# A two-layer hybrid decoder trunk on one core: weights fetched two groups ahead, queries and keys copied out of PSUM, two tiles transposed by DMA

## The chip, the core and the metric

The kernel runs on one core of a Trainium2 chip. The core has five engines, each with a queue of its own that it works off in order: TensorE (PE in the profile: matmuls, and PEld for its weight loads), VectorE (DVE), ScalarE (ACT), GpSimd (POOL) and SyncE (SP, which here only issues transfers). Sixteen DMA engines move data. Operands lie in SBUF; matmuls write to PSUM, of which this kernel uses banks of 128 x 512 float32. The metric is the device time of one execution in microseconds.

## The reference, cut

Two layers; a sequence of 512 tokens with 2048 features, float32. Each layer:

```python
h = rmsnorm(x, norm_g);  proj = h @ w_in            # 2048 x 7696
cv_h, cv_b, cv_c, cv_g, sb_q, sb_k, sb_v, sb_g, gl_q, gl_k, gl_v, gl_g, gl_lr = split(proj)
y_conv = cv_b * (causal conv of width 3 over cv_c * cv_h, + bias) * silu(cv_g)
q, k = rmsnorm per head of 128 (sb_q), (sb_k)       # 8 heads
w = exp(log_sigmoid(z) + later)                     # z = q k^T, strictly causal; later: the sum of
y_sb = (w @ sb_v) * silu(sb_g)                      #   log_sigmoid(-z) over later keys of the row
g = log_sigmoid(gl_lr @ gla_w_up + gla_b_up) / 16
y_gla = rmsnorm(gated linear attention(gl_q, gl_k, gl_v, g)) * silu(gl_g)    # 4 heads
x = x + concat(y_conv, y_sb, y_gla) @ w_out         # 2048 x 2048
```

## The kernel before

**Splitting.** Every float32 operand of a large matmul is split into two float16 parts (hi and lo), and three products (hi hi, hi lo, lo hi) take the place of one float32 product.

**Groups.** `specs` lists the column groups of 256 in the order of their use: per layer 6 groups for linear attention (GLA: values, one with the 16 low-rank columns, queries, keys, two gates), 4 for the first half of the convolution, 16 for stick-breaking attention (four times values, gate, queries, keys, for two heads each), 4 for the rest of the convolution, and 8 of `w_out`. A group is 192 matmuls of 256 columns or 96 of 512. Each is fetched and prepared in two halves of 1024 rows, h = 0 and 1:

- `fetch` issues the transfer on SP into a buffer of the pool `stage` (tile `st`, 3 buffers, so one and a half groups);
- `wmax` (L322) squares the half on ACT and sums (tile `junk` takes the squares); `wscale` (L332 to L353) makes a power of two from the sums, on POOL and DVE;
- `whi` (L393) writes the hi part on ACT, `wlo` (L400) the lo part on DVE, into pool `wpool` (tiles `wh`, `wl`, 3 buffers each). `wlo` is the last reader of the staged half.

`weights()` is called at the head of each group's matmuls; it calls `load` for the group itself if that isn't done, and for the next one.

**Matmuls.** `project_cols` (L558 to L560) makes a group's output by columns, `project_toks` (L566 to L568) by tokens, in two PSUM banks out of three (`psp`), `project_by_token` (L591) one token tile after the other, for the first two groups of a layer and for the last of the first layer.

**Order.** But for the start, where the order of ACT and DVE is written out by hand, a scheduler of the framework sets each engine's order at build time from its own model of time and from priorities; `high_priority` lifts what is called in it. Semaphores then hold each instruction back until its data are there.

**GLA.** For each of two head pairs (`p`), seven levels of VectorE and ACT work (L760 to L778: exponentials, splits L724 and L733 on ACT, L725 and L734 on DVE) feed small matmuls (L739); then L817 and L818 split the carried attention, and L830 applies it to the values. These stand among the next groups' matmuls on PE.

**Stick-breaking attention.** `attend` leaves four pieces per two heads (`scores` and `values` of each) that `go()` starts one by one within the following groups. `scores` ends in L956 (exponential, ACT), L959 and L960 (hi and lo) and four DMA transposes on SP (L962, tile `th`), which `values` needs for L978. For queries and keys, ACT squares each 128 x 128 block out of PSUM with an accumulated sum (L1023, eight a group), `rsqrt` follows on ACT and DVE, and DVE multiplies from PSUM into `raw` (L1032 queries, L1040 keys); only then are the group's banks free. `raw` is split into `qp` and transposed by DMA (L1050).

**Change of layer.** In the last group of `w_out`, `finish` (L1070) writes a token tile's new x, and `xprep` prepares it for the next layer: `xnorm`, `xgain` (L446, both halves), `xhigh` (eight float32 transposes on PE, L456, and the hi part out of PSUM on ACT, L458), `xlow` (L465, the lo part on DVE). The results `xh`, `xl` are what the next layer's matmuls read.

Of the kernel before, what the change touches and what calls it, by code (L numbers as in the profile page):

```python
# [6 lines left out]
F16 = mybir.dt.float16  # L7
# [10 lines left out]
P = 128  # L18
# [16 lines left out]
def hybrid_trunk(ctx, tc, x, norm_g, w_in, conv_w, conv_b, sb_qn_g, sb_kn_g,  # L35
# [30 lines left out]
    def sm(n, tag, bufs=None):  # L66
        return small.tile([P, n], F32, tag=tag, name=nm(tag), bufs=bufs)

    def wk(shape, tag, bufs=None, dt=F32):
        return work.tile(shape, dt, tag=tag, name=nm(tag), bufs=bufs)  # L70
# [33 lines left out]
    epst = const.tile([P, 1], F32, tag="epst", name="epst")  # L104
    V.memset(epst, EPS)

    colno = wk([P, P], "gy", 1)
    V.tensor_tensor_scan(colno, ones.to_broadcast([P, P]), ones.to_broadcast([P, P]), -1.0, ALU.mult, ALU.add)
    parno = wk([P, 32], "raw", 1)
    V.transpose(parno, colno[:, :32])  # L110
# [176 lines left out]
    cursor = [0]  # L287

    def load(i):
        if i < 3:  # L290
            load_(i)
        else:
            with tc.high_priority():
                load_(i)

    staged, peak, scales = {}, {}, {}

# [19 lines left out]
    def wmax(i, h):  # L317

        n = sum(c[1] for c in specs[i][2])
        if h == 0:  # L320
            peak[i] = sm(2, "wm")
        S.activation(junk(HK * n).rearrange("p (k n) -> p k n", k=HK), staged[i][h][:, :, :n], AF.Square,  # L322
                     accum_out=peak[i][:, h:h + 1])
# [51 lines left out]
    def whi0(h, q, eng):  # L375
# [9 lines left out]
        else:  # L385
            V.tensor_scalar(wh[:, ks, :GW], staged[0][h][:, ks, :GW], scales[0][0], None, ALU.mult)

    def whi(i, h):
        n = sum(c[1] for c in specs[i][2])
        wh = wpool.tile([P, HK, GX], F16, tag="wh", name=nm("wh"))  # L390
        wl = wpool.tile([P, HK, GX], F16, tag="wl", name=nm("wl"))
        for ks, s_ in wparts(i, h):
            S.activation(wh[:, ks, :n], staged[i][h][:, ks, :n], AF.Copy, scale=s_)  # L393
        loaded[i][0].append((wh, wl))

    def wlo(i, h):
# [5 lines left out]

    def load_(i):

        fetch(i)
        for h in range(2):
            wmax(i, h)
        wscale(i)
        for h in range(2):
            whi(i, h)  # L410
            wlo(i, h)

    def weights():

        i = cursor[0]
        cursor[0] += 1
        for j in (i, i + 1):
            if j < len(specs) and j not in loaded:
                load(j)
        return loaded.pop(i)  # L420

    fetch(0)
# [47 lines left out]

    def xprep(l, t, dst):

        xnorm(l, t)
        for h in range(2):
            xgain(t, h)
            xhigh(t, h, dst)
            xlow(t, h, dst, False)

    def halves(tag):

# [61 lines left out]
    for l in range(depth):  # L542
# [53 lines left out]
        def gate(ps, u, mx=None):  # L596

            g = wk([P, 2, seq], "g")
            for c in range(2):
                y = wk([P, seq], "gy", 1)  # L600
                S.activation(y, ps[c], AF.Copy, scale=u)
                a = wk([P, seq], "ga")
                S.activation(a, y, AF.Abs)
                S.activation(a, a, AF.Exp, scale=-1.0)
                S.activation(a, a, AF.Ln, bias=1.0)
                V.scalar_tensor_tensor(a, y, 0.0, a, ALU.min, ALU.subtract)
                S.activation(a, a, AF.Exp)
                V.tensor_tensor(g[:, c, :], y, a, ALU.mult)
            if mx is not None:
                V.tensor_reduce(mx, g, AX.XY, ALU.max, apply_absolute_value=True)  # L610
            return g
# [55 lines left out]
        for p in range(2):  # L667
# [4 lines left out]
            S.activation(a, gp, AF.Abs, bias=bcol)  # L672
            S.activation(a, a, AF.Exp, scale=-1.0)
            S.activation(a, a, AF.Ln, bias=1.0)
            r_ = wk([P, seq], "gy", 1)
            S.activation(r_, gp, AF.Relu, bias=nbu[:, l, p:p + 1], scale=-1.0)
            V.tensor_tensor(a, a, r_, ALU.add)
            for t in range(NT):
# [313 lines left out]
        for j in range(4):  # L992
# [22 lines left out]
            qkT = []  # L1015
            for gain in (None, kg[:, l, :]):
                ps, u = project_toks(xh, xl)
                sq = sm(8, "qs")
                raw = wk([P, NT, GW], "raw", 1)
                for t in range(NT):  # L1020
                    for hh in range(2):
                        o = (t % 2) * GW + hh * P
                        S.activation(raw[:, t, hh * P:(hh + 1) * P], ps[t // 2][:, o:o + P], AF.Square,  # L1023
                                     accum_out=sq[:, 2 * t + hh:2 * t + hh + 1])
                u2 = sm(1, "qu2")
                V.tensor_scalar(u2, u, u, 1.0 / P, ALU.mult, ALU.mult)
                rs = sm(8, "qr")
                rsqrt(rs, sq, u2, 8, "q")
                V.tensor_scalar(rs, rs, u, None, ALU.mult)
                if gain is None:  # L1030
                    for b in range(2):
                        V.tensor_tensor(raw[:, 2 * b:2 * b + 2, :].rearrange("p a (h c) -> p (a h) c", c=P),  # L1032
                                        ps[b].rearrange("p (a c) -> p a c", c=P),
                                        rs[:, 4 * b:4 * b + 4].rearrange("p (a o) -> p a o", o=1).to_broadcast([P, 4, P]),
                                        ALU.mult)
                else:
                    for t in range(NT):
                        for hh in range(2):
                            o = (t % 2) * GW + hh * P
                            V.scalar_tensor_tensor(raw[:, t, hh * P:(hh + 1) * P], ps[t // 2][:, o:o + P],  # L1040
                                                   rs[:, 2 * t + hh:2 * t + hh + 1], gain, ALU.mult, ALU.mult)

                top = 2.0 ** 10 if gain is None else 1.0
                parts = wk([P, 2, NT * GW], "qp", 1, F16)
# [76 lines left out]
```

## Time and profile before

| | |
|---|---|
| median of 3 runs | 1791.44 us (1789.22 to 1795.85) |
| the profiled execution | 1791.4 us |
| its span in the profile | 1789.6 us |
| granted TensorE clock, mean | 0.996 |
| busy: PE / DVE / ACT / POOL | 1742.9 / 1049.7 / 1085.9 / 55.1 us |
| moved by DMA | 202.61 MB, 113 GB/s on average |

A row of a group of instructions reads: line, engine, operation, tile written <- tiles read, shapes, count | busy us, mean ns of one | idle time of the engine just before them, and what ended most of it. A row of waits reads: waiting instruction <- what released it: us in total, times, longest. A row of the timeline: start us, us, instruction, and in brackets the idle time before it. A row of stages: start and end, length, then busy us (and instructions) of PE, weight loads, DVE, ACT, POOL, then granted clock, DMA share, GB/s. Times are from the span's start.

### The profile page before, as it was taken

The numbers are of one execution on the slowest core, as the hardware profiler recorded it, in microseconds if no ns is written. First come the engines' busy times: TensorE is split into PE (matmuls) and PEld (weight loads), VectorE is DVE, ScalarE is ACT, GpSimd is POOL, SyncE is SP. The second block draws the span as 40 slices with busy tenths as digits, with TensorE's granted clock in tenths as the row PEclk, the third lists the DMA queues.
The fourth block names the chain that finished last, engine by engine and source line by source line (L and its number), as shares of the span: only waits on it lengthen the run. The fifth ranks groups of instructions, "written<-read, shape, count | busy, mean of one in ns | idle before, by whom it ended". The sixth has DMA issues, their size and how long they took to land. (4 is left out here: it accounts for less than half of the span.)

```text
span 1789.6 us, 30839 instructions
## 1 busy us (share of the span) xinstructions
PE 1742.9 (97%) x12878; PEld 1238.4 (69%) x12878; DVE 1049.7 (59%) x1991; ACT 1085.9 (61%) x1652; POOL 55.1 (3%) x104
## 2 busy tenths in 40 slices
PE   8999999999999999999999999999999999999999
PEld 6644456777777754788985454568686778548888
DVE  7556677656565647544463566875666565564323
ACT  8557576567676766555555674775766666655431
POOL 2000000000000000000010000000000000000000
PEclk9999999999999999999999999999999999999999
DMA  6322222243535355444423322223444435444441
GB/s 216 118 95 94 86 80 83 83 119 106 137 92 151 86 150 123 143 148 144 142 89 102 117 73 71 95 80 98 123 119 121 98 108 124 117 124 142 142 142 48
DMA packets 257675, 202.61 MB, mean 113 GB/s; under 512 B 84658, under 2 KB 256764, under 8 KB 257024
## 3 DMA queue, kind: packets, MB, share of 16 engines
q1 hardware_dynamic: 248528, 191.19, 37.4%
q10 hardware_dynamic: 9008, 9.45, 1.6%
q8 instruction: 101, 1.65, 0.4%
q14 instruction: 38, 0.31, 0.1%
HBM read 173.36 MB, written 8.39 MB: 102 GB/s over the span
## 5 line engine op out<-in xcount | busy, mean ns | idle before, releaser
L322 ACT ACTIVATE junk<-st 128x2048 uint8<-128x2048 f32 (+1 forms) x150 | 287.4, 1916 | 339.9 <-DMA st<-in_w_in_dram 244.1
L566 PE MATMUL psp<-wh,m 128*128 128x256 f16 x1664 | 454.3, 273 | 2.4 <-DVE raw L1032 1.7
L567 PE MATMUL psp<-wl,m 128*128 128x256 f16 x1664 | 454.3, 273 | 0.0
L568 PE MATMUL psp<-wh,m 128*128 128x256 f16 x1664 | 454.2, 273 | 0.0
L400 DVE SCALAR_TENSOR_TENSOR wl<-st,ws,wh 128x2048 f16<-128x2048 f32 (+1 forms) x120 | 282.1, 2353 | 147.9 <-ACT wh L393 142.1
L393 ACT ACTIVATE wh<-st,ws 128x2048 f16<-128x2048 f32 (+1 forms) x118 | 236.0, 2001 | 93.8 <-PE psp L568 59.1
L566 PE MATMUL psp<-wh,x 128*128 128x256 f16 x768 | 209.4, 273 | 2.0 <-DVE raw L1032 1.7
L567 PE MATMUL psp<-wl,x 128*128 128x256 f16 x768 | 209.3, 273 | 0.0
L568 PE MATMUL psp<-wh,x 128*128 128x256 f16 x768 | 209.3, 273 | 0.0
L558 PE MATMUL psp<-x,wh 128*128 128x512 f16 x512 | 194.1, 379 | 0.0
L558 PE MATMUL psp<-m,wh 128*128 128x512 f16 x512 | 194.1, 379 | 0.0
L559 PE MATMUL psp<-x,wh 128*128 128x512 f16 x512 | 194.0, 379 | 0.0
L559 PE MATMUL psp<-m,wh 128*128 128x512 f16 x512 | 194.0, 379 | 0.0
L560 PE MATMUL psp<-x,wl 128*128 128x512 f16 x512 | 193.8, 379 | 0.0
L560 PE MATMUL psp<-m,wl 128*128 128x512 f16 x512 | 193.7, 379 | 0.0
L560 PEld LDWEIGHTS <-wl 128*128 128x128 f16 x1024 | 100.2, 98 | 123.2 <-issue 4.5
L559 PEld LDWEIGHTS <-wh 128*128 128x128 f16 x1024 | 100.2, 98 | 117.6 <-issue 2.3
L558 PEld LDWEIGHTS <-wh 128*128 128x128 f16 x1024 | 100.2, 98 | 117.2 <-issue 2.0
L566 PEld LDWEIGHTS <-m 128*128 128x128 f16 x1664 | 163.0, 98 | 23.2 <-DVE raw L1032 2.3
L567 PEld LDWEIGHTS <-m 128*128 128x128 f16 x1664 | 163.0, 98 | 21.0 <-issue 2.1
L568 PEld LDWEIGHTS <-m 128*128 128x128 f16 x1664 | 163.1, 98 | 20.4 <-issue 1.4
L333 DVE TENSOR_SCALAR wq<-wgm 128x1 f32<-128x1 f32 x75 | 16.0, 213 | 263.9 <-POOL wgm L332 263.9
(278 smaller groups left out, 2325.7 us busy)
## 6 DMA issues: line engine op xcount, KB each, us to landing
st<-in_w_in_dram SPq DMA_DIRECT2D x120, 1024.0 KB, 5.3
st<-in_w_out_dram SPq DMA_DIRECT2D x32, 1024.0 KB, 5.8
x<-in_x_dram SPq DMA_DIRECT2D x4, 1024.0 KB
qT<-in_x_dram ACTq DMA_DIRECT2D x8, 512.0 KB, 4.9
qT<-xs ACTq DMA_DIRECT2D x8, 512.0 KB
xs<-x SPq DMA_DIRECT2D x14, 256.0 KB, 4.6
out_dram<-kT SPq DMA_DIRECT2D x14, 256.0 KB, 4.2
th<-za SPq DMA_TRANSPOSE x64, 5.5
```

What stands on the lines that cost most here:

```text
L322: S.activation(junk(HK * n).rearrange("p (k n) -> p k n", k=HK), staged[i][h][:, :, :n], AF.Square, accum_out=peak[i][:, h:h + 1])
L333: V.tensor_scalar(m, gm[:, 0:1], gm[:, 1:2], 2.0 ** -120, ALU.add, ALU.max)
L393: S.activation(wh[:, ks, :n], staged[i][h][:, ks, :n], AF.Copy, scale=s_)
L400: V.scalar_tensor_tensor(wl[:, ks, :n], staged[i][h][:, ks, :n], s_, wh[:, ks, :n], ALU.mult, ALU.subtract)
L558: T.matmul(o, wh[:, kk, cs], xh[:, :, k, :], start=st_, stop=False)
L559: T.matmul(o, wh[:, kk, cs], xl[:, :, k, :], start=False, stop=False)
L560: T.matmul(o, wl[:, kk, cs], xh[:, :, k, :], start=False, stop=en)
L566: T.matmul(o, ah[:, t, k, :], wh[:, kk, :n], start=st_, stop=False, skip_group_check=True)
L567: T.matmul(o, ah[:, t, k, :], wl[:, kk, :n], start=False, stop=False, skip_group_check=True)
L568: T.matmul(o, al[:, t, k, :], wh[:, kk, :n], start=False, stop=en, skip_group_check=True)
```

## The change

`weights()` now calls `fetch` for the group after the next, and `load` for the next group no longer fetches. `load_` puts both squares of a group behind the last `whi` of the group before it on ACT (`issue_after`), and all loads are at high priority. Queries and keys are copied out of PSUM by ACT, 512 columns at a time, squared from the copy, and summed by a reduction on DVE; the multiplications then read and write `raw`. In `xprep` the first two of four token tiles are split in SBUF and transposed by eight DMAs, in buffers of `th`, `raw` and `qp`. `gate` works in place in its output tile, and the tile `gy` is gone; its other uses take `th` and `za`.

```diff
     def load(i):
-        if i < 3:
+        with tc.high_priority():
             load_(i)
-        else:
-            with tc.high_priority():
-                load_(i)
...
         for ks, s_ in wparts(i, h):
-            S.activation(wh[:, ks, :n], staged[i][h][:, ks, :n], AF.Copy, scale=s_)
+            lasthi[i] = S.activation(wh[:, ks, :n], staged[i][h][:, ks, :n], AF.Copy, scale=s_)
...
     def load_(i):
-        fetch(i)
-        for h in range(2):
-            wmax(i, h)
+        with tc.issue_after(lasthi[i - 1].ins):
+            for h in range(2):
+                wmax(i, h)
         wscale(i)
...
-        for j in (i, i + 1):
-            if j < len(specs) and j not in loaded:
-                load(j)
+        if i + 2 < len(specs):
+            with tc.high_priority():
+                fetch(i + 2)
+        if i and i + 1 < len(specs):
+            load(i + 1)
         return loaded.pop(i)
...
         for h in range(2):
             xgain(t, h)
-            xhigh(t, h, dst)
-            xlow(t, h, dst, False)
+            if t >= NT // 2:
+                xhigh(t, h, dst)
+                xlow(t, h, dst, False)
+                continue
+            xv = xt[t // 2][:, t % 2, h * (D // 2):(h + 1) * (D // 2)]
+            parts = wk([P, 2, D // 2], *((("raw", 1), ("qp", 1))[h] if t else ("th", 2)), F16)
+            S.activation(parts[:, 0], xv, AF.Copy)
+            V.tensor_tensor(parts[:, 1], xv, parts[:, 0], ALU.subtract)
+            for i in range(2):
+                nc.sync.dma_start_transpose(dst[i][:, t, h * HK:(h + 1) * HK, :], parts[:, i])
...
-                y = wk([P, seq], "gy", 1)
+                y = g[:, c, :]
...
-                for t in range(NT):
-                    for hh in range(2):
-                        o = (t % 2) * GW + hh * P
-                        S.activation(raw[:, t, hh * P:(hh + 1) * P], ps[t // 2][:, o:o + P], AF.Square,
-                                     accum_out=sq[:, 2 * t + hh:2 * t + hh + 1])
+                for b in range(2):
+                    rb = raw[:, 2 * b:2 * b + 2, :]
+                    S.activation(rb, ps[b].rearrange("p (a c) -> p a c", a=2), AF.Copy)
+                    e = wk([P, 2 * GW], "e")
+                    S.activation(e, rb.rearrange("p a c -> p (a c)"), AF.Square)
+                    V.tensor_reduce(sq[:, 4 * b:4 * b + 4], e.rearrange("p (a c) -> p a c", c=P), AX.X, ALU.add)
```

The order of the engines moves with it. The changed kernel's line numbers differ: squares are L319, `whi` L392, L817 is L827, L807 is L817, L733 is L743, L1073 is L1081, the fetch L308, the new DMA transposes L487.

ACT, layer 0, end of the first GLA head pair, before:

```order
L733 ACTIVATE m_409<-qT_1084 64x4x64 x2
L322 ACTIVATE junk_2521,wm_2518<-st_2516 128x2048
L724 ACTIVATE m_409<-e_1754 128x256
L733 ACTIVATE m_409<-e_1754 64x4x64 x2
L733 ACTIVATE m_409<-e_1769 64x4x64 x2
L393 ACTIVATE wh_2402<-st_2380,ws_2392 128x8x256
L807 ACTIVATE m_410<-zw_1547 128x256 x4
L817 ACTIVATE za_1792<-psz_1795 128x512
L817 ACTIVATE e_1794<-psz_1805 128x512
L322 ACTIVATE junk_2666,wm_2665<-st_2661 128x2048
L817 ACTIVATE za_1793<-psz_1795 128x512
```

And after:

```order
L743 ACTIVATE m_409<-e_1754 64x4x64 x2
L743 ACTIVATE m_409<-e_1769 64x4x64 x2
L817 ACTIVATE m_410<-zw_1547 128x256 x3
L392 ACTIVATE wh_2402<-st_2251,ws_2392 128x8x256
L319 ACTIVATE junk_2519,wm_2518<-st_2378 128x2048
L817 ACTIVATE m_410<-zw_1547 128x256
L319 ACTIVATE junk_2521,wm_2518<-st_2380 128x2048
L827 ACTIVATE za_1792<-psz_1795 128x512
L827 ACTIVATE e_1794<-psz_1805 128x512
L827 ACTIVATE za_1793<-psz_1795 128x512
```

The two squares of a group now follow the second half's split, ahead of the three splits of the carried attention. At the end of the second head pair, ACT after the change:

```order
L392 ACTIVATE wh_3054<-st_2801,ws_3044 128x8x256
L319 ACTIVATE junk_3189,wm_3188<-st_3030 128x2048
L827 ACTIVATE za_2143<-psz_2146 128x512
L319 ACTIVATE junk_3191,wm_3188<-st_3032 128x2048
L827 ACTIVATE e_2145<-psz_2156 128x512
L827 ACTIVATE za_2144<-psz_2146 128x512
```

There the second square stands between the splits. ACT, layer 1, scores of a fourth head, before:

```order
L1023 ACTIVATE raw_14767,qs_14766<-psp_14572 128x128 x4
L322 ACTIVATE junk_15110,wm_15109<-st_15105 128x2048
L956 ACTIVATE zw_14507<-zw_14507 128x896
L393 ACTIVATE wh_14841<-st_14821,ws_14835 128x8x256
L1023 ACTIVATE raw_14767,qs_14766<-psp_14573 128x128 x3
L956 ACTIVATE zw_14532<-zw_14532 128x384
```

And after (L966 is L956, L1033 and L1035 the copy and the square of the queries):

```order
L392 ACTIVATE wh_14514<-st_14287,ws_14504 128x8x256
L319 ACTIVATE junk_14771,wm_14770<-st_14490 128x2048
L319 ACTIVATE junk_14773,wm_14770<-st_14492 128x2048
L1033 ACTIVATE raw_14713<-psp_14518 128x512
L1035 ACTIVATE e_14715<-raw_14713 128x512
L966 ACTIVATE zw_14453<-zw_14453 128x896
L966 ACTIVATE zw_14478<-zw_14478 128x384
```

Two squares stand ahead of the exponentials where one of a later half stood. SP at the change of layer, before:

```order
L1073 DMA xs<-x_7573 128x256
L311 DMA st_9735<-in_w_in_dram 128x8x256
L311 DMA st_9735<-in_w_in_dram 128x8x16
L1073 DMA xs<-x_7573 128x256
L1073 DMA xs<-x_7574 128x256
L311 DMA st_9968<-in_w_in_dram 128x8x256
L1073 DMA xs<-x_7574 128x256
```

And after (the tiles `m_409` and `m_410` are the next layer's `xh` and `xl`):

```order
L1081 DMA xs<-x_7557 128x256
L487 DMA_TRANSPOSE m_409<-th_9414 128x8x128
L487 DMA_TRANSPOSE m_409<-th_9420 128x8x128
L308 DMA st_9319<-in_w_in_dram 128x8x256
L308 DMA st_9319<-in_w_in_dram 128x8x16
L1081 DMA xs<-x_7557 128x256
L487 DMA_TRANSPOSE m_410<-th_9414 128x8x128
L487 DMA_TRANSPOSE m_410<-th_9420 128x8x128
L1081 DMA xs<-x_7558 128x256
L487 DMA_TRANSPOSE m_409<-raw_9493 128x8x128
L487 DMA_TRANSPOSE m_409<-qp_9499 128x8x128
L308 DMA st_9694<-in_w_in_dram 128x8x256
```

The eight transposes stand among the weight halves and the writes of x (the last two follow after one more write).

More of the change, by code (lines that the diff above doesn't have):

```diff
@@ L105, in hybrid_trunk @@
     V.memset(epst, EPS)
-    colno = wk([P, P], "gy", 1)
+    colno = wk([P, P], "th", 2)
     V.tensor_tensor_scan(colno, ones.to_broadcast([P, P]), ones.to_broadcast([P, P]), -1.0, ALU.mult, ALU.add)
@@ L386, in whi0 @@
             V.tensor_scalar(wh[:, ks, :GW], staged[0][h][:, ks, :GW], scales[0][0], None, ALU.mult)
+    lasthi = {}
     def whi(i, h):
@@ L607, in gate @@
                 S.activation(a, a, AF.Exp)
-                V.tensor_tensor(g[:, c, :], y, a, ALU.mult)
+                V.tensor_tensor(y, y, a, ALU.mult)
             if mx is not None:
@@ L674, in hybrid_trunk @@
             S.activation(a, a, AF.Ln, bias=1.0)
-            r_ = wk([P, seq], "gy", 1)
+            r_ = wk([P, seq], "za")
             S.activation(r_, gp, AF.Relu, bias=nbu[:, l, p:p + 1], scale=-1.0)
@@ L1030, in hybrid_trunk @@
                 if gain is None:
[L1031 to L1035, printed above, removed]
+                    r8 = raw.rearrange("p a (h c) -> p (a h) c", c=P)
+                    V.tensor_tensor(r8, r8, rs.rearrange("p (a o) -> p a o", o=1).to_broadcast([P, 8, P]), ALU.mult)
                 else:
@@ L1038, in hybrid_trunk @@
                         for hh in range(2):
-                            o = (t % 2) * GW + hh * P
-                            V.scalar_tensor_tensor(raw[:, t, hh * P:(hh + 1) * P], ps[t // 2][:, o:o + P],
-                                                   rs[:, 2 * t + hh:2 * t + hh + 1], gain, ALU.mult, ALU.mult)
+                            rp = raw[:, t, hh * P:(hh + 1) * P]
+                            V.scalar_tensor_tensor(rp, rp, rs[:, 2 * t + hh:2 * t + hh + 1], gain, ALU.mult, ALU.mult)
                 top = 2.0 ** 10 if gain is None else 1.0
```

## The prediction, on record before the run

> **What bounds the kernel now.** I read the page's busy times first, then a table of stages, then who TensorE waited for, then the timeline around single waits.
>
> ```profile
> PE 1742.9 (97%) x12878; PEld 1238.4 (69%) x12878; DVE 1049.7 (59%) x1991; ACT 1085.9 (61%) x1652; POOL 55.1 (3%) x104
> ```
>
> TensorE (PE) is the bound: 1789.6 - 1742.9 = 46.7 us of the span are idle. A change that leaves its matmuls alone has no more to win than that, plus what stops cost beside their idle time. The stages (start and end, length, PE busy, ..., granted clock in the third column from the right):
>
> ```profile
> 0.00:66.00 66.00, 56.89 (x423) 45.02 (x424) 47.88 (x127) 47.00 (x57) 10.63 (x13) 0.97 0.59 192
> 180.00:345.00 165.00, 155.81 (x1042) 96.45 (x1040) 116.37 (x231) 100.86 (x161) 2.91 (x7) 0.99 0.26 84
> 435.00:665.00 230.00, 226.31 (x1794) 172.33 (x1792) 137.10 (x245) 151.88 (x251) 4.73 (x12) 1.00 0.47 118
> 880.00:960.00 80.00, 76.56 (x655) 65.18 (x653) 46.36 (x85) 44.30 (x59) 8.62 (x6) 0.98 0.27 82
> 1050.00:1215.00 165.00, 155.28 (x1030) 92.05 (x1029) 123.05 (x254) 106.05 (x169) 3.31 (x8) 1.00 0.27 84
> 1310.00:1530.00 220.00, 213.87 (x1753) 169.14 (x1752) 134.69 (x231) 142.48 (x241) 4.33 (x11) 0.99 0.46 118
> ```
>
> Idle by stage: start-up 9.1; the two linear-attention (GLA) stages 9.2 and 9.7; the two stick-breaking stages 3.7 and 6.1; the change of layer 3.4. The rest of the span holds 5.5 us. Whom PE waited for, over the whole span:
>
> ```profile
> PE psm L978 <- DMA th<-za: 6.4, 6, 3.6
> PE psz L739 <- ACT m L733: 5.2, 9, 1.9
> PE psz L830 <- ACT za L817: 5.0, 4, 1.6
> PE psz L739 <- DVE m L734: 3.6, 7, 0.7
> PE psp L566 <- DVE raw L1032: 3.4, 6, 0.6
> PE psz L830 <- DVE e L818: 3.4, 2, 1.7
> PE psp L591 <- ACT wh L393: 3.2, 1, 3.2
> ```
>
> L739 and L830 are the GLA matmuls, L978 applies the attention weights, L566 begins a projection, L591 is the layer's start. ScalarE (ACT) is named often. What holds it:
>
> ```profile
> ACT junk L322 <- DMA st<-in_w_in_dram: 244.1, 90, 9.5
> ACT junk L322 <- DMA st<-in_w_out_dram: 94.8, 20, 8.6
> ACT wh L393 <- PE psp L568: 69.7, 26, 5.4
> ```
>
> ACT stands 338.9 us in front of the squares (L322) of a weight half that has not landed, and all that is queued behind a square stands with it. Three places show this reaching PE. GLA, layer 0:
>
> ```profile
> 206.50 0.58 ACT L817 ACTIVATE e<-psz 128x512 f16<-128x512 f32 x1
> 212.85 1.91 ACT L322 ACTIVATE junk<-st 128x2048 uint8<-128x2048 f32 x1 [5.77 <-DMA st<-in_w_in_dram]
> 214.76 0.58 ACT L817 ACTIVATE za<-psz 128x512 f16<-128x512 f32 x1
> 215.39 0.27 PE L830 MATMUL psz<-za,v 128*128 128x256 f16 x1 [1.65 <-ACT za L817]
> ```
>
> The last L817 could have followed its neighbour at 207.1; a square stood between, and PE lost 1.65 us. Attention, layer 1:
>
> ```profile
> 1411.01 1.91 ACT L322 ACTIVATE junk<-st 128x2048 uint8<-128x2048 f32 x1 [9.49 <-DMA st<-in_w_in_dram]
> 1412.92 0.94 ACT L956 ACTIVATE zw<-zw 128x896 f32<-128x896 f32 x1
> 1421.08 0.27 PE L978 MATMUL psm<-th,v 128*128 128x256 f16 x1 [3.58 <-DMA th<-za]
> ```
>
> The exponential L956 came after the square, so the transposes of its result came late. The layer's change:
>
> ```profile
> 929.37 1.91 ACT L322 ACTIVATE junk<-st 128x2048 uint8<-128x2048 f32 x1 [5.55 <-DMA st<-in_w_in_dram]
> 931.28 2.09 ACT L393 ACTIVATE wh<-st,ws 128x2176 f16<-128x2176 f32 x1
> 933.43 4.58 PE L591 MATMUL psp<-wh,m 128*128 128x272 f16 x24 [3.20 <-ACT wh L393]
> 940.62 2.02 PE L591 MATMUL psp<-wh,m 128*128 128x272 f16 x16
> 906.84 1.04 PE L456 MATMUL psz<-ident,x 128*128 128x128 f32 x8
> 907.71 1.04 PE L591 MATMUL psp<-wl,m 128*128 128x256 f16 x8
> ```
>
> Two prices beside the idle time: eight 256-column matmuls last 1.04 us, the last of them 0.27 (row of 215.39), so they follow each other every (1.04 - 0.27) / 7 = 0.11 us (the transposes of L456 too), and each stop costs 0.27 - 0.11 = 0.16 us more than its idle. After a long stop the clock is lower: 24 matmuls took 4.58 us after 3.20 us of idle, where 16 take 2.02, so 24 about 2.96: 1.6 us lost.
>
> **The change, part by part.**
>
> *Squares behind the preceding split, fetch two groups ahead.* No work is added or removed. The staging pool keeps three halves, one and a half groups, so the second half of group i+1 still starts only when the split of group i's first half (L393, then L400) frees its buffer. What moves is ACT's place for the squares: both now stand after the split of group i's second half. That split waits for PE to finish with a weight buffer, about half a group after the first half's split; one group is 192 matmuls of 0.11, 21 us. From the freed buffer a transfer takes:
>
> ```profile
> st<-in_w_in_dram SPq DMA_DIRECT2D x120, 1024.0 KB, 5.3
> th<-za SPq DMA_TRANSPOSE x64, 5.5
> L400 DVE SCALAR_TENSOR_TENSOR wl<-st,ws,wh 128x2048 f16<-128x2048 f32 x116 | 272.2, 2348 | 146.5 <-ACT wh L393 140.7 <-PE psz L936 5.7
> ```
>
> 2.3 + 5.3 = 7.7 us against some 10 us between the two splits: in the steady course the half lies in SBUF before its square is due. I take most of ACT's 338.9 us as gone; what that is worth is read stage by stage.
>
> GLA: waits on L733 5.2 (9 stops), on L817 and L818 5.0 + 3.4 = 8.4 (6 stops), on VectorE's L734 3.6 (7 stops). Of the first I take 4 us away; of the second half, 4.2, since in the second head pair a square still stands between two L817 in the new order; of the third 1, since VectorE is not relieved. With some 12 stops fewer at 0.16: 4 + 4.2 + 1 + 1.9 = 11 us. Ends: 0 if the order of the ping-pong and not the late transfer makes these stops; 18.9 idle + 22 stops x 0.16 = 22 if all go.
>
> Attention: of the 6.4 on L978 I take 4.8 away (the 3.6 and a part of the rest; the transposes themselves still take 5.5 us to land). With four stops, 5.4 us. Ends 0 and 7.4.
>
> Change of layer: the 3.20 and the 1.6 behind it, 4.8 us, because L393 no longer stands behind the square of a later group. Ends 0 and 4.8.
>
> *Queries and keys copied out of PSUM.* On ACT, per group, 8 squares with their accumulator reads go, 2 copies and 2 squares come; on VectorE 2 reductions of 128x512 come:
>
> ```profile
> L1023 ACT ACTIVATE raw<-psp 128x128 f32<-128x128 f32 x128 | 33.3, 271 | 9.8 <-PE psp L568 8.2 <-DVE wu L353 1.7
> L1023 ACT ACTIVATION_READ_ACCUMULATOR raw<-psp 128x1 f32 x128 | 26.1, 204 | 0.0
> L869 ACT ACTIVATE qT<-psp,wu 128x512 f32<-128x512 f32 x8 | 5.4, 674 | 0.1
> L838 ACT ACTIVATE e<-za 128x512 f32<-128x512 f32 x8 | 5.0, 627 | 11.5 <-DVE za L836 9.1 <-DVE e L847 2.4
> L693 DVE TENSOR_REDUCE qTmx<-psp 128x1 f32<-128x512 f32 x4 | 2.8, 692 | 3.7 <-PE psp L560 3.7
> ```
>
> ACT: 33.3 + 26.1 = 59.4 becomes 32 x (0.67 + 0.63) = 41.6, 18 us less. VectorE: 32 x 0.69 = 22 us more, beside PE, in stages where it is busy 137 of 230 us; without that cover a head's chain would be 1.4 us later. The multiplications (L1032, L1040) stay, on SBUF. The gain on PE: the bank is free after the copy, no longer after the root and L1032, so the six waits on L1032 go: 3.4 + 6 x 0.16 = 4.4 us. Ends 3.4 and 4.4: the next group needs the bank 48 matmuls, 5.2 us, after its start, and the first bank is complete as long before the group's end.
>
> *Two input tiles transposed by DMA.* 32 transposes leave PE, 32 x 0.11 = 3.5 us; the four PSUM evictions and subtractions on ACT and VectorE become equal ones on SBUF, counted nothing. SP gains 8 transposes:
>
> ```profile
> L962 SPq DMA_TRANSPOSE th<-za x64: 1196/1380/3583, 405.5 to 1597.8; - x64
> DMA to landing us min/median/max: 2.9/5.5/7.9
> ```
>
> 8 x 1.4 = 11 us of SP, in a queue with the weight fetches and the writes of x. In the new order the low halves of tile 0 stand behind a weight half and the write of tile 1, and those of tile 1 behind the next half and the write of tile 3. The high halves are issued while PE still works on the old layer's last group (21 us); the low halves are the ones that can be late, by as much as the landing itself varies. I set 2 us of new waiting, near that spread (7.9 - 5.5 = 2.4). Ends: 0, and 11 (all of SP's issue time on PE's path).
>
> [...]
>
> *gate in place, other tags.* The second gate copy no longer waits for one buffer; PE never waited for that, so nothing.
>
> Sum: 11 + 5.4 + 4.8 + 4.4 + 3.5 - 2 = 27. The profiled execution took 1791.4 us (span 1789.6), the median of the runs is 1791.44: **1764 us**. Start-up, the same instructions in the same order up to the second group, stays.
>
> **The rivals.**
>
> 1. *The GLA stops are the ping-pong's own.* ACT and VectorE alternate through seven levels there, VectorE is busy 116 and 123 of 165 us, and PE's order fixes where it asks. For it: the seven waits on L734, and the stops of nearly equal size in all four head pairs. Against: the rows of 206.50 to 215.39. Then GLA gives 0 and L978 half: 2.7 + 4.8 + 4.4 + 3.5 - 2 = 13, 1778 us.
> 2. *The fetch is not ahead.* Three buffers bound it. If wherever the two splits come close together the square waits as before, both GLA and L978 give nothing and the layer's change half: 2.4 + 4.4 + 3.5 - 2 = 8, 1783 us.
> 3. *PE waits for the DMA transposes.* With 11 us in place of 2: 1773 us.
> 4. *Slower: ACT held by the split.* The second half's split waits for PE (69.7 us in 26 waits, 2.7 each, in the row above), and the two squares, 2 x 1.9, now stand together behind it, ahead of the scores' exponentials (L956). PE waits for those through L978. If PE felt half of these 2.7 + 3.8 = 6.5 us in each of the 16 heads, it would be 16 x 3.25 = 52 us more: 1816. It decides from 27 / 16 = 1.7 us a head. Against it: L956 waits for VectorE's work on the scores in any case, which leaves ACT time for two squares; and the one square at 1411.01 held L956 by waiting for its data, not by its 1.9 us.
>
> **How the numbers follow.** Forecast 0.55, rival 1 0.17, rival 2 0.11, rival 3 0.10, rival 4 0.07. A measurement of this kernel tells some 0.5%, 9 us, from no change: the forecast and rival 3 lie below 1782.4, rival 1 in three cases of four (0.13), rival 2 in four of eleven (0.04), with 0.01 of it slower. Faster 0.82, same 0.10, slower 0.08. The range: from all ends good (22 + 7.4 + 4.8 + 4.4 + 3.5 = 42, 1749) to rival 2: 1748 to 1784.
>
> **What would show it.** Squares that wait for DMA well under 100 us in total; no wait of L566 on the queries' multiplication; L978 under 2 us; no 3 us stop at the layer's change, but perhaps waits of L591 on DMA; GLA idle near 9 for both stages together. It is wrong if the squares' waits go and PE's idle in GLA does not, or if L978's waits grow.

## The result and the profile after

The changed kernel takes **1742.56 us** (median of 4 runs, 1742.25 to 1742.75), the kernel before 1792.48 beside it (4 runs, 1789.22 to 1795.85): a ratio of 0.9721, 95% interval 0.9702 to 0.974. That is 50 us, where 27 were forecast; 1742.56 lies below the range's lower end, 1748. The direction was right, the size was not.

The profiled execution spans 1740.9 us. Its busy line, from the page:

```profile
PE 1726.8 (99%) x12846; PEld 1232.4 (71%) x12846; DVE 1068.9 (61%) x2015; ACT 1090.0 (63%) x1460; POOL 75.1 (4%) x104
```

PE is idle for 1740.9 - 1726.8 = 14.1 us, where it was 46.7. ACT is as busy as before (1085.9), and VectorE busier. The stages, with the same columns as in the prediction:

```profile
0.00:66.00 66.00, 58.33 (x424) 45.76 (x425) 48.11 (x127) 45.11 (x55) 10.65 (x13) 1.00 0.60 195
180.00:345.00 165.00, 165.00 (x1173) 107.95 (x1172) 125.42 (x242) 109.62 (x163) 3.02 (x7) 1.00 0.29 89
435.00:665.00 230.00, 230.00 (x1746) 167.77 (x1745) 147.06 (x251) 154.27 (x187) 10.66 (x13) 1.00 0.45 120
880.00:960.00 80.00, 77.22 (x552) 53.86 (x550) 47.21 (x87) 44.60 (x52) 11.04 (x7) 1.00 0.43 120
1050.00:1215.00 165.00, 165.00 (x1220) 113.01 (x1219) 123.23 (x239) 110.00 (x160) 3.42 (x8) 1.00 0.29 89
1310.00:1530.00 220.00, 220.00 (x1625) 155.83 (x1623) 142.63 (x232) 150.20 (x180) 10.26 (x12) 1.00 0.46 121
```

In both GLA stages and both attention stages PE is busy without a gap, and the granted clock is 1.00 throughout. What is left of PE's waits, the whole list (line and tile, what was waited for, us in total, times, longest):

```profile
PE psz L210 <- DVE identb L192: 3.7, 1, 3.7
PE psp L601 <- DMA m<-raw: 2.0, 1, 2.0
PE psz L457 <- DVE x L447: 1.7, 2, 0.9
PE psp L601 <- ACT wh L381: 1.5, 1, 1.5
PE psz L457 <- DVE x L466: 1.3, 1, 1.3
PE psp L601 <- ACT x L459: 0.2, 1, 0.2
```

All of it is start-up or change of layer. Every wait of GLA, of L978 and of the projections on L1032 is gone. On ACT, the groups of the squares (L319 here) and of the weight splits (L392): busy us, mean ns, then the idle time in front of them and what ended it:

```profile
L319 ACT ACTIVATE junk<-st 128x2048 uint8<-128x2048 f32 (+1 forms) x150 | 285.5, 1903 | 7.6 <-DMA st<-in_w_out_dram 4.5 <-DMA st<-in_w_in_dram 1.2
L392 ACT ACTIVATE wh<-st,ws 128x2048 f16<-128x2048 f32 (+1 forms) x118 | 236.3, 2003 | 202.6 <-PE psp L569 100.9 <-PE psp L578 73.9 <-PE psp L601 10.5
L392 ACT ACTIVATE wh<-st,wsr 128x512 f16<-128x512 f32 x128 | 81.6, 710 | 100.5 <-PE psp L578 74.4 <-DVE wu L348 15.0 <-DVE wsr L347 11.1
```

The squares wait for data 6 us in place of 339. But ACT has not got that time: it now stands 202.6 + 100.5 = 303 us in front of the splits, mostly until PE is done with a weight buffer. It stands nearly as long as before, in another place and for another partner. The same corner of GLA as in the prediction (there L830 lost 1.65 us):

```profile
197.88 1.89 ACT L319 ACTIVATE junk<-st 128x2048 uint8<-128x2048 f32 x1
199.77 0.40 ACT L817 ACTIVATE m<-zw 128x256 f16<-128x256 f32 x1
200.08 1.89 ACT L319 ACTIVATE junk<-st 128x2048 uint8<-128x2048 f32 x1
201.97 0.57 ACT L827 ACTIVATE za<-psz 128x512 f16<-128x512 f32 x1
203.43 0.60 ACT L827 ACTIVATE za<-psz 128x512 f16<-128x512 f32 x1 [0.41 <-DVE za L828]
```

Two squares stand ahead of L827 here, with no idle time in front of either, and PE does not stop. At the end of the second head pair a square still stands between two L827, and it has its data too:

```profile
295.07 0.57 ACT L827 ACTIVATE za<-psz 128x512 f16<-128x512 f32 x1
295.54 1.90 ACT L319 ACTIVATE junk<-st 128x2048 uint8<-128x2048 f32 x1
297.44 0.58 ACT L827 ACTIVATE e<-psz 128x512 f16<-128x512 f32 x1
```

How long each stretch lasts can be read from the first starts of two lines of PE, the first GLA transpose of a layer (L739 before, L749 after) and its first score matmul (L934, L944). Layer 0, before and after:

```profile
L739 PE MATMUL psz<-m x216: 216/219/379, 158.9 to 314.0; 128*128 128x128 f16 x84, 128*128 128x256 f16 x20, 128*128 128x512 f16 x4
L934 PE MATMUL psz<-kT,qT x96: 219/300/379, 386.8 to 687.3; 128*128 128x512 f16 x24, 128*128 128x384 f16 x24, 128*128 128x128 f16 x24, 128*128 128x256 f16 x24
L749 PE MATMUL psz<-m x216: 218/220/380, 158.0 to 294.8; 128*128 128x128 f16 x84, 128*128 128x256 f16 x20, 128*128 128x512 f16 x4
L944 PE MATMUL psz<-kT,qT x96: 218/299/380, 371.4 to 667.2; 128*128 128x512 f16 x24, 128*128 128x384 f16 x24, 128*128 128x128 f16 x24, 128*128 128x256 f16 x24
```

GLA with the work up to the first score took 386.8 - 158.9 = 227.9 us and takes 213.4. Cut in this way at the first starts (and at the last start of L978, at the end of attention), the kernels give these stretches, in us, from PE's first matmul to the start of its last (227.8 where the rows' rounding gives 227.9). The kernels under the first two are the experiments of the next section:

| kernel | to GLA | GLA 0 | attention 0 | to GLA 1 | GLA 1 | attention 1 | end |
|---|---|---|---|---|---|---|---|
| before | 155.3 | 227.8 | 345.3 | 309.0 | 227.0 | 349.2 | 168.4 |
| after | 154.3 | 213.4 | 340.6 | 303.3 | 213.4 | 340.7 | 167.6 |
| fetch part alone | 154.0 | 213.4 | 340.6 | 305.2 | 213.4 | 340.7 | 167.6 |
| PSUM copies alone | 155.0 | 232.0 | 366.3 | 309.7 | 231.0 | 366.6 | 170.0 |
| squares moved in GLA only | 154.8 | 213.4 | 346.7 | 307.4 | 213.4 | 348.7 | 167.6 |
| squares moved elsewhere only | 153.9 | 227.7 | 340.7 | 305.2 | 227.7 | 340.7 | 167.6 |
| squares twice | 157.7 | 216.0 | 340.6 | 310.9 | 216.0 | 340.7 | 167.6 |
| two staging halves | 153.8 | 216.5 | 349.8 | 301.5 | 216.7 | 348.1 | 168.1 |

From before to after: GLA 28.0, attention 13.2, the change of layer 5.7, start and end 1.8. The two stages that the forecast sized at 11 and 5.4 us gave 41.

### The profile page after: what moved, and what is told of

Same layout as the page of the kernel before. It is cut to its first block, busy times and chain, and to the rows that moved or that the text cites. A ratio compares the mean times of both kernels' runs of the same rounds, so it can differ in the third digit from the quotient of the medians.

```text
span 1740.9 us, 30651 instructions
## 1 busy us (share of the span) xinstructions
PE 1726.8 (99%) x12846; PEld 1232.4 (71%) x12846; DVE 1068.9 (61%) x2015; ACT 1090.0 (63%) x1460; POOL 75.1 (4%) x104
## 3 DMA queue, kind: packets, MB, share of 16 engines
q8 instruction: 100, 1.64, 0.4%
## 4 chain that ended last, share of the span: by engine, by line
PE 48%; issue 7%; DVE 1%; DMA 1%; SPq 0%; POOL 0%; ACT 0%; POOLq 0%; DVEq 0%
PE psp L576 8%; PE psp L578 8%; PE psp L577 8%; PE psp L570 6%; PE psp L568 6%; PE psp L569 6%; PE psp L601 3%; PE psz L749 1%; PE psm L988 1%; PE psz L944 1%; PE psz L840 0%; DMA m<-raw 0%; DVE wl L399 0%; SPq L487 0%; DMA xs<-x 0%
## 5 line engine op out<-in xcount | busy, mean ns | idle before, releaser
L392 ACT ACTIVATE wh<-st,ws 128x2048 f16<-128x2048 f32 (+1 forms) x118 | 236.3, 2003 | 202.6 <-PE psp L569 100.9
L319 ACT ACTIVATE junk<-st 128x2048 uint8<-128x2048 f32 (+1 forms) x150 | 285.5, 1903 | 7.6 <-DMA st<-in_w_out_dram 4.5
L392 ACT ACTIVATE wh<-st,wsr 128x512 f16<-128x512 f32 x128 | 81.6, 710 | 100.5 <-PE psp L578 74.4
```

Of the source, the lines that this page charges most:

```text
L392: lasthi[i] = S.activation(wh[:, ks, :n], staged[i][h][:, ks, :n], AF.Copy, scale=s_)
```

## The experiments

Theory A: ACT's squares, standing in its queue until their weights landed, caused nearly all stops of PE; once they stand where their data are there, all stops go. Its rivals: the prediction's sizes (B); the PSUM copies did part of it (C); in attention TensorE merely asks later (D); any holding of ACT costs by its length (E); the place of a square in ACT's order counts, not its data (F).

### Each part alone

**Fetch and squares only.** The hunks of `load`, `load_`, `weights` and `lasthi`:

```diff
-        fetch(i)
-        for h in range(2):
-            wmax(i, h)
+        with tc.issue_after(lasthi[i - 1].ins):
+            for h in range(2):
+                wmax(i, h)
...
+        if i + 2 < len(specs):
+            with tc.high_priority():
+                fetch(i + 2)
+        if i and i + 1 < len(specs):
+            load(i + 1)
```

> The kernel before with one part of the change: weights fetched two groups ahead and a group's squares queued behind the preceding group's split; no PSUM copies, no DMA transposes, gate as before. Theory A (squares that stood on ScalarE waiting for their weights caused nearly every stop of TensorE in GLA, in attention and at the layer's change): GLA's 19 us of idle, the 6.4 us of L978 and the 3.2 us of L591 go with what each stop costs beside its idle, so about 38 to 43 us: 1750 to 1755 us, squares' DMA waits under 30 us, waits of L566 on L1032 unchanged at about 3.4 us. Theory B (the prediction's sizes: GLA 11, L978 5.4, change of layer 4.8): 21 us, 1771 us, with half of the waits of L830 left. Theory C (the PSUM copies, by relieving ScalarE, removed the rest): 1765 to 1775 us, GLA idle near 9 us until the copies come in.

1744.6 us, before 1791.38; ratio 0.9735 (0.9714 to 0.9755). Of the 50 us this part carries 47. Its PE waits hold neither GLA nor L978, and the 3.4 us on L1032, which theory A expected to stay, went too, without any copy. Theory A's mechanism held, with a time 5 us below its range; B and C did not.

**Copies out of PSUM only.** The hunks at `raw` and `sq`:

```diff
-                        S.activation(raw[...], ps[t // 2][:, o:o + P], AF.Square, accum_out=sq[...])
+                    S.activation(rb, ps[b].rearrange(...), AF.Copy)
+                    S.activation(e, rb.rearrange(...), AF.Square)
+                    V.tensor_reduce(sq[:, 4 * b:4 * b + 4], ..., AX.X, ALU.add)
```

> The kernel before with queries and keys copied out of PSUM, and nothing else of the change. Theory A: only the waits of L566 on the queries' multiplication go (3.4 us and the six stops' cost): 1786 to 1789 us; squares still wait some 330 us. Theory C (a relieved ScalarE is what removed the attention and GLA stops): 1770 to 1780 us. A loss, if the two reductions of VectorE a group lie on the attention's chain: over 1795 us.

1837.15 us, ratio 1.0249 (1.0221 to 1.0277): **46 us slower**. Only the last case named there, over 1795 us, points this way, and the reductions of VectorE that it names are the smaller part of what the rows show. In the profiled execution PE's idle time grew from 46.7 to 1838.2 - 1759.8 = 78.4 us and its busy time by 16.9, at a granted clock of 0.984 against 0.996: part of the loss is the lower clock. PE's waits have a new first row, and ACT's timeline at the first of these stops shows what the scores (L934) waited for:

```profile
PE psz L934 <- DMA kT<-qp: 38.0, 15, 5.8
```

```profile
370.30 1.91 ACT L322 ACTIVATE junk<-st 128x2048 uint8<-128x2048 f32 x1 [3.59 <-DMA st<-in_w_in_dram]
372.21 0.58 ACT L1023 ACTIVATE raw<-psp 128x512 f32<-128x512 f32 x1
372.69 1.99 ACT L393 ACTIVATE wh<-st,ws 128x2048 f16<-128x2048 f32 x1
374.58 0.58 ACT L1023 ACTIVATE raw<-psp 128x512 f32<-128x512 f32 x1
382.56 1.91 ACT L322 ACTIVATE junk<-st 128x2048 uint8<-128x2048 f32 x1 [3.64 <-DMA st<-in_w_in_dram]
386.37 1.04 ACT L1043 ACTIVATE qp<-raw 128x1024 f16<-128x1024 f32 x1
390.63 0.43 PE L934 MATMUL psz<-kT,qT 128*128 128x512 f16 x2 [1.91 <-DMA kT<-qp]
```

Each link of the keys' chain (copy, square, reduction, root, split L1043) takes a place of its own in ACT's queue. One square that waits for weights stands ahead of the copies here, and another, with a split behind it, ahead of L1043; so the keys' transposes come late. These two waits are 3.59 and 3.64 us; for the reduction, ACT's root waits 2.08 us in between. The same copies beside squares that do not wait cost nothing (below).

**DMA transposes only.** The hunks of `xprep`:

```diff
+            S.activation(parts[:, 0], xv, AF.Copy)
+            V.tensor_tensor(parts[:, 1], xv, parts[:, 0], ALU.subtract)
+                nc.sync.dma_start_transpose(dst[i][:, t, h * HK:(h + 1) * HK, :], parts[:, i])
```

> The kernel before with the input tiles 0 and 1 transposed by DMA, and nothing else of the change. Prediction's size: 3.5 us less for the 32 transposes, up to 2 us of new waiting at the layer's change, and there the square still stands in front of the split, so the DMA may be hidden: 1788 to 1791 us. Rival (TensorE waits for the DMA transposes behind the weights on SP): 1796 us or more, with waits of L591 on DMA over 8 us.

1786.13 us, 0.9961 (0.9947 to 0.9976): 5.2 us less, 1.9 beyond the expected 1788; the rival's 1796 is out. PE waits 1.9 us for a transposed tile here, while its wait of 3.2 us for a split (L591 on L393) falls to 1.0.

**Gate in place and tags only** (`y = g[:, c, :]` in place of a buffer of its own):

> The kernel before with the gate multiplied in place and the temporaries' tags moved, and nothing else. Prediction and theory A: no change, 1790 to 1794 us. Rival (the single buffer of the gate's copy held ScalarE's queue and with it the scaled GLA operands): 5 us or more faster.

1792.83 us, 1.0008 (0.9991 to 1.0024): nothing, as predicted.

### The changed kernel less one part

These four ran beside one another (before: 1795.8).

> The changed kernel once more, to stand beside the next three kernels, which differ from it by one part each. All theories: 1742 to 1743 us.

1742.21 us, 0.9704 (0.9689 to 0.9718).

Without the copies (the hunk above reversed):

> The changed kernel without the PSUM copies (queries and keys normalised from PSUM as before). The fetch part alone gave 1744.6 us with no wait of a projection on the queries' multiplication left, so by theory A the copies are worth nothing once the squares come late: 1741 to 1743 us, with no wait of L576's successor on the multiplication. Theory C2 (the copies alone cost 46 us, so some of that cost is still inside the changed kernel, beside other work): 1730 to 1738 us. The prediction's size (4.4 us won by the copies): 1747 us.

1742.49 us, 0.9704 (0.969 to 0.9718): the copies are worth 0.3 us, within the runs' spread. C2 and the prediction's 4.4 both fall.

Without the DMA transposes:

> The changed kernel with all input tiles transposed by TensorE. Prediction's size: 32 transposes of 0.11 us come back and the 2.0 us of waiting for the transposed tile go: 1744 us (1743.5 to 1745). If the DMA transposes carry more than that (the alone part won 5.2 us): 1746 to 1748 us. If the DMA wait at the layer's change outweighs them: under 1742 us.

1744.91 us (1744.65 to 1745.16), the first case: the DMA transposes carry 2.7 us. The 32 transposes of 3.5 us return, and the wait on the transposed tile goes, but 1.7 us of waits of the input projection on the eviction (L459) come in its place.

With the last writes of x on ACT's queue:

```diff
-            nc.sync.dma_start(to[t * P:(t + n) * P, cs]...
+            (nc.sync if gi < NG - 1 or last else S).dma_start(to[t * P:(t + n) * P, cs]...
```

> The changed kernel with the last writes of x in layer 0 (L1081, the last w_out group) issued on ScalarE's queue in place of SyncE's, so that they no longer stand behind the two pieces of a weight half there. Theory: the 2.0 us that VectorE's gain (L447) waited for that write and the 2.0 us that the input projection waited for the last transpose belong together and both go: 1739.5 to 1741 us. Rival: the transposes themselves (3.3 to 3.9 us to land, issued about 1.3 us apart on SyncE) set that wait, and in the new order a weight half is issued ahead of them: 1742 to 1746 us, with the wait of L601 on DMA at 2 us or more.

1742.24 us: the same. VectorE's 2.0 us on the write went, but the input projection then waits for the DMA transposes three times, 1.1, 1.0 and 0.6 us. The rival held: the wait at the change of layer is the transposes' own.

### Where the squares cost, place by place

The fetch part again, with the squares queued behind the split only in the GLA stages; the complement has `not` in its condition. Against the fetch part:

```diff
-        with tc.issue_after(lasthi[i - 1].ins):
+        if 7 <= i % 38 < 16:
+            with tc.issue_after(lasthi[i - 1].ins):
...
+        else:
```

> The fetch part alone, with the squares queued behind the preceding split only for the groups whose squares fall in the two GLA stages (groups 7 to 15 of each layer); all other squares as in the kernel before. Theory A (each place loses what its own late squares cost): GLA's 19 us of idle and the slower matmuls behind its stops go, 25 to 29 us: 1763 to 1767 us; the waits of L978 (some 6 us) and L591 (3.2 us) stay. The prediction's size for GLA, 11 us: 1781 us. If the stages do not add up (what is won in GLA is lost behind it): over 1785 us.

> The complement: squares queued behind the preceding split everywhere but in the GLA stages. Theory A: GLA keeps its 19 us of idle, while attention, the change of layer and the projections between lose theirs, 18 to 21 us: 1770 to 1775 us. With the sizes predicted for these places (5.4 + 4.8): 1781 us.

1765.89 us, 0.9844 (0.9825 to 0.9863), and 1772.12 us, 0.9884 (0.9867 to 0.9902), before 1794.27. The gains are 28.4 and 22.2 us, together a little more than the fetch part's 46.8 beside another run of the kernel before; in the table the gains of the stretches add up to within 1.5 us (30.0 and 18.5 against 47.1): with the squares moved in GLA alone, GLA takes 213.4 us as after, and attention stays within 1.5 us of before; the complement gives the reverse. Each place lost what its own late squares cost.

**TensorE asks later.** The order after has one more difference in attention: in the kernel before, the first of a second head's 18 value matmuls (L978) stands after 96 of the 192 matmuls of the keys' projection, and after, all 18 stand behind the 192. The six stops of L978 were all at that one matmul. So the kernel before, with that alone (`lastmm` is the projection's last matmul):

```diff
+            def behind(hh):
+                with tc.issue_after(lastmm[0].ins):
+                    values(hh)
```

> The kernel before, with one thing moved: TensorE multiplies the attention weights of a pair's second head (L978) behind all 192 matmuls of the keys' projection, where the kernel before has the first of these 18 matmuls after 96 of them. Every other queue keeps its order and squares stay late. Theory D (in attention the stop came from where TensorE asks, and the changed kernel asks 96 matmuls, 10.5 us, later): the six waits of L978 go, 6.4 us with 1 us beside and the lower clock behind them: 1780 to 1785 us. Theory A (late squares alone): the wait moves with the question, L978 keeps 3 us or more, 1788 us or more.

1797.46 us, 1.0023 (1.0009 to 1.0037): no gain. The waits of L978 went, but PE's first row is now a wait that had been 3.4 us, and the timeline shows what it waits behind (L1030, L1039 are L1023, L1032 of before):

```profile
PE psp L568 <- DVE raw L1039: 15.2, 6, 3.6
```

```profile
1422.15 1.91 ACT L322 ACTIVATE junk<-st 128x2048 uint8<-128x2048 f32 x1 [8.55 <-DMA st<-in_w_in_dram]
1426.79 0.25 ACT L1030 ACTIVATE raw<-psp 128x128 f32<-128x128 f32 x1
1430.49 0.21 ACT L183 ACTIVATE qr<-qr 128x8 f32<-128x8 f32 x1
1433.15 0.27 PE L568 MATMUL psp<-wh,m 128*128 128x256 f16 x1 [3.55 <-DVE raw L1039]
```

D fell, and A's number for L978 was a miss as well: the wait did not move with the question but to the next one. The late square holds the queries' squares of the second bank and the root as it held the exponential; by these rows, L978's stop had been covering that wait.

**Fetch ahead, squares left.** The fetch part without its queueing; the hunk is against that part. Every queue then holds the same instructions in the same order as in the kernel before.

```diff
-        with tc.issue_after(lasthi[i - 1].ins):
-            for h in range(2):
-                wmax(i, h)
+        for h in range(2):
+            wmax(i, h)
```

> The kernel before with the fetch two groups ahead and in high priority, but the squares not queued behind the preceding split. Theory: with three staging halves the buffers set when a fetch starts, so this alone is nothing: 1790 to 1795 us, squares' DMA waits near 339 us. Rival (the depth of the fetch makes the squares early): under 1770 us.

1793.69 us, 1.0002 (0.9987 to 1.0018): nothing. The earlier fetch alone moves nothing; the gain needs the squares' new place. No run has that place without the earlier fetch, so whether the queueing would do alone is open.

### Holding, place or data

These four ran beside one another (before: 1796.13).

**Every square issued twice** in the changed kernel (`for _ in range(2):` around it):

> The changed kernel with every square issued twice: ScalarE gets 150 more instructions of 1.9 us, 286 us of work, nearly as much as the 339 us that the squares of the kernel before waited. Theory A (a wait for data costs because it comes when the chain behind it is due; work that the order allows for costs little): under 1755 us. Rival E (ScalarE held is ScalarE held, 47 us for 339): 1742 + 286 x 47 / 339 = 1782 us.

1757.07 us, 0.978 (0.9761 to 0.9798): ACT is busy 1359.7 us, 77% of the span, and that costs 14.6 us against the changed kernel with four halves that ran beside it (1742.47, below). E would have had 40. By the table the cost stands in GLA (2.6 us each), at the change of layer (7.6) and at the start (3.4).

**Four staging halves, squares not queued behind the split** (gate in place, `bufs=4`):

> The kernel before (with the gate in place, which measured as nothing and makes room) with four staging halves in place of three; the squares are not queued behind the preceding split, but a half's transfer can start half a group earlier. Theory A (late data): squares' DMA waits under 100 us, 1743 to 1755 us. Rival F (the place of the squares in ScalarE's order is what counts): 1780 us or more although the squares no longer wait.

1803.5 us, 1.0034 (1.0017 to 1.0052). This does not tell A from F: with the buffer free sooner the scheduler put the squares about half a group further ahead, and they still wait 277 us, not the under 100 that A had expected:

```profile
L322 ACT ACTIVATE junk<-st 128x2048 uint8<-128x2048 f32 (+1 forms) x150 | 287.1, 1914 | 277.3 <-DMA st<-in_w_in_dram 206.3
```

What it shows is that a further buffer is no cure while the order lets the squares run ahead of their data.

**Two staging halves** in the changed kernel (`bufs=2`):

> The changed kernel with two staging halves in place of three: a half's transfer (5.3 us) starts only when the split of the same half of the preceding group is done, so squares wait again although they are queued behind the split. Theory A: squares' DMA waits over 150 us and stops of TensorE back: 1765 us or more. Rival F (place, not data): 1742 to 1750 us.

```profile
L319 ACT ACTIVATE junk<-st 128x2048 uint8<-128x2048 f32 (+1 forms) x150 | 286.7, 1911 | 298.1 <-DMA st<-in_w_in_dram 232.1
PE psz L944 <- DMA kT<-qp: 9.7, 8, 2.5
```

1763.8 us, 0.9818 (0.9803 to 0.9834). Late data are back, and 21 us with them (1763.8 - 1742.47), a little under theory A's 1765, in GLA and with stops at the scores in attention. In ACT's queue the squares run on average 1.5 halves ahead of the splits here, as in the changed kernel; it is 2.6 in the kernel before and 3.4 in the one with four halves. So late data cost 21 us without the old place. The kernel before lost 47 by 339 us of waiting in the squares' old places; whether the place itself counts beside the data is open, because each edit also moves other instructions by some places.

**Four staging halves** in the changed kernel:

> The changed kernel with four staging halves. Theory A: nothing but 8 us of squares' DMA waits is left to win, and TensorE is idle 14 us in all, 9 of them at the start: 1739 to 1743 us. A gain of over 4 us would mean that the start is bound by the staging buffers.

1742.47 us, 0.9702 (0.9685 to 0.9719): as after. No version here beats the changed kernel by more than its runs scatter; the fetch part alone comes within some 2 us of it.

## Why the prediction was right and wrong

*What bounds the kernel.* PE, and the stops were rightly tied to ACT's squares. That 46.7 us was the most that could be won, "plus what stops cost beside their idle time", held: idle fell by 32.6 us, 32 transposes (3.5) went, and 48.7 - 32.6 - 3.5 = some 13 us came from beside the idle. Two terms were too small. The forecast took some 19 us of idle away (9.2 in GLA, 4.8 at L978, 3.2 at the change of layer, 3.4 at L1032, less 2 of new waiting), where 32.6 went; most of the rest is GLA's. And it counted about 5 us beside the idle, where 13 came.

The second term alone puts the time below the range. With all ends good the sum takes 31.9 us of idle away, nearly what went, but 7 beside it. The prediction charged 0.16 us a stop and let the clock count only "after a long stop", at the layer's change (0.64 from 933.40 to 938.10). In the trace of before the clock also fell after two other stops, one in GLA of layer 0 and one in attention of layer 1 (last section); at 0.61 for 1.90 us and 0.52 for 2.00, the latter lost 0.39 x 1.90 + 0.48 x 2.00 = 1.7 us. Start-up had 0.97 too, against 1.00 after. But GLA of layer 1 ran at 1.00 and still gave 13.6 us for 9.7 of idle. What its stops cost beside idle and clock is not shown by a run.

*GLA, 11 us with an upper end of 22; measured 28.0.* The steps that failed are "of the second half, 4.2, since in the second head pair a square still stands between two L817" and "of the third 1, since VectorE is not relieved". A square does stand between two L827 afterwards (row of 295.54), but it has its data and takes 1.9 us, which the order leaves room for; what had mattered was the idle time in front of it. The waits named after VectorE went too, with VectorE as busy as ever (116 and 123 us before, 125 and 123 after). For the split L818 the trace of before shows why: at 215.37 it had waited 2.29 us for ACT's L817. That ACT also held L734 is inferred from its waits being gone. Rival 1, the ping-pong's own stops, is refuted by 165.00 of 165.00.

*Attention, 5.4 with an upper end of 7.4; measured 13.2.* The mechanism was right, the exponential behind the square. Of the 13.2, 9.8 are the idle time of both stages. Missing were the clock after the 3.58 us stop, some 1.7 us, and that the same square also holds the queries' root, so that the 3.4 us of waits on L1032 belong to this term.

*Queries and keys, 4.4 with ends 3.4 and 4.4; measured 0.* The step that failed is "the bank is free after the copy, ... so the six waits on L1032 go". They went with the squares, without a copy. The lower end of 3.4 excluded a loss, and alone the copies cost 46 us: the longer chain was costed as hidden, but its links were not placed in ACT's queue among the waiting squares. The prediction names that queue and did not walk this chain through it. The 18 us that ACT was to save are not there either: ACT is busy 1090.0 us with the copies and 1083.8 without them. The squares with their reads followed each other every 0.25 us in the trace before, since the records of the accumulator's reads overlap those of the squares, and the two durations had been added:

```profile
360.70 0.27 ACT L1023 ACTIVATE raw<-psp 128x128 f32<-128x128 f32 x1
360.86 0.20 ACT L1023 ACTIVATION_READ_ACCUMULATOR raw<-psp 128x1 f32 x1
360.95 0.28 ACT L1023 ACTIVATE raw<-psp 128x128 f32<-128x128 f32 x1
```

*Change of layer, 4.8; DMA transposes, 3.5 less 2.* The fetch part took 3.8 us from that stretch, and the transposes carry 2.7 in place of 1.5. The new wait came where it was set, 2.0 us on a low half (first list above), but it replaces 1.7 us that PE waited there for evictions. The eight transposes were issued from 869.7 us on, and PE had the last one it waited for at 894.67.

*Right as they stood:* that three halves leave the fetch no further ahead (fetch ahead alone 1.0002), that the gate is worth nothing, and that rival 4, ACT held by the split, would not come: ACT stands 303 us in front of the splits and PE loses nothing by it.

## What to carry to other kernels

In a queue that works in order, look at what stands behind an instruction that waits for a transfer, and price all of that by its own dates, not only the stop that the profile names; here one row of ACT, 339 us in front of squares, answered for stops of PE at five other lines. If a cause is common to many stops, take the stops with it as all gone in one case of the sum; here that case had the idle time right and only the price beside it too small, so look in the trace for what each stop costs behind it, the granted clock above all. And cost a change that adds links to a chain in the state that it will meet: the copies were worth 0 beside early squares and minus 46 us beside late ones.

## What the runs showed of the hardware

The lower clock after a stop, in the trace of before, by short windows (PE's busy time first, granted clock third from the right):

```profile
1417.30:1421.10 3.80, 0.22 (x3) 0.05 (x1) 3.70 (x9) 2.23 (x5) 0.00 (x0) 1.00 0.41 71
1421.10:1423.00 1.90, 1.33 (x7) 0.82 (x8) 1.33 (x3) 0.50 (x1) 0.00 (x0) 0.61 1.00 289
1423.00:1425.00 2.00, 2.00 (x11) 1.44 (x10) 1.23 (x1) 0.56 (x1) 0.00 (x0) 0.52 1.07 281
1425.00:1428.00 3.00, 3.00 (x30) 2.68 (x29) 0.07 (x1) 2.60 (x8) 0.40 (x1) 1.00 1.51 126
```

```profile
1423.18 0.42 PE L566 MATMUL psp<-wh,m 128*128 128x256 f16 x1
1423.39 0.42 PE L567 MATMUL psp<-wl,m 128*128 128x256 f16 x1
```

After 3.58 us without a matmul, and 0.57 more behind a single L978, 256-column matmuls start every 0.21 us until 1425, then every 0.11 again. The busy share hides this: PE reads 2.00 of 2.00 at a clock of 0.52. It also happens after less, in GLA:

```profile
212.58 0.83 PE L830 MATMUL psz<-m,v 128*128 128x128 f16 x12
216.71 1.49 PE L830 MATMUL psz<-m,v 128*128 128x128 f16 x12
217.00:221.00 4.00, 4.00 (x29) 3.05 (x27) 3.96 (x5) 0.23 (x1) 0.00 (x0) 0.62 0.02 4
```

The same twelve matmuls take 0.83 us ahead of two stops of 1.65 and 0.46 us, and 1.49 behind them. But the same two stops in layer 1, 1.64 and 0.46 us, left the clock alone, at 1.00 from 1098 to 1102:

```profile
1098.22 0.27 PE L830 MATMUL psz<-za,v 128*128 128x256 f16 x1 [1.64 <-ACT za L817]
1099.49 0.83 PE L830 MATMUL psz<-m,v 128*128 128x128 f16 x12
```

So the lower clock can follow stops of this size and need not; no run shows what decides. In shorter windows of that trace the clock reads 0.50 from 1421.90 to 1424.80 and from 216.70 to 220.00, which agrees with 0.21 us in place of 0.11; in layer 0 it came with 2.1 us of idle in two pieces.

Not expected either: the 64 DMA transposes of L978's operand, which landed in 5.5 us (median) before, land in 3.6 after, with the same shapes. The traces give a landing for only ten and nine of the 64. The median goes with the squares' place in attention: 3.2 us with the squares moved elsewhere only, 5.2 with them moved in GLA only. Why is left open.

```profile
th<-za SPq DMA_TRANSPOSE x64, 3.6
```
